# Output projection with five head pairs by seven products, small products in pieces of 32, and single-source mixer work on ScalarE

## The chip, the core and the metric

The kernel runs on one core of one Trainium2 chip. TensorE does the products, VectorE and ScalarE the elementwise work, GpSimd a few accumulating transfers, and SyncE's queue issues nearly all transfers. The metric is the device time of one execution in microseconds. Before the change the median of three runs is 973.27 us, from 970.83 to 974.09. A measurement of this kernel can tell a change of about 0.3%, some 2.9 us, from none.

## The reference

One decoder layer on 512 tokens of width 2048, behind 16 learned meta tokens; everything is float32:

```
x = rms_norm(input) ; p = x @ w_in                 # one projection, columns split among three mixers
A: gated DeltaNet, 6 heads x 128 (conv, SiLU, l2 norm, chunked delta rule)
B: GLA linear attention, 5 heads (dk 64, dv 128), key-dim gate, chunked
C: forgetting attention, 5 heads x 128, blocks of 128 queries
each head: o * silu(z)                             # A and B with a head norm first
y = concat(A 768, B 640, C 640) @ w_out + input    # one output projection, 2048 x 2048
out = rms_norm(y) without the meta tokens
```

The concatenated width is 16 heads of 128. The kernel counts it in eight **pairs** `kp` of two heads: pairs 0 to 2 are the DeltaNet heads, 3 and 4 the first four GLA heads, 5 is GLA head 4 with attention head 0, and 6 and 7 are the other four attention heads.

## The kernel before, in words

**Products.** Every large operand is split into a high and a low part (`wh`/`wl`, `oh`/`ol`, `sh`/`sl`): ScalarE copies the high part, VectorE subtracts it from the source to get the low one. A large product is then three matmuls (high by high, low by high, high by low), 128 rows by up to 512 columns. Products between small float32 tiles run without the split, and the trace has two matmuls for each of them.

**Order.** Every instruction is recorded at one line (L283, in `Weave.emit`) in an order that a planner at build time chooses. Each piece of work is a Python generator; what it yields, an operation or a list of operations, is emitted as a whole. The planner keeps a modelled clock for each engine, gives each generator a priority, and among those whose operands are modelled as ready takes the earliest. TensorE has two modes, full matmuls and small ones (fewer than 128 rows or 64 columns); the planner stays in the small mode for `LIGHT` us of modelled time and in the full one for at least `HEAVY`. `BACK` bounds how far the modelled transfer queue may run ahead of TensorE. On the chip every engine then executes its own list strictly in that order.

**Stages on TensorE.** The input projection's first columns (`pz`, `px`) run to about 540 us. From there to 823 us the three mixers are interleaved with the rest of the input projection (`pbfq`, `pbgz`, `pbfz`: 128x512 matmuls, the bulk that fills TensorE while a mixer's chains run on other engines) and with the first blocks of the output projection (`po`). The small products `pss` belong to GLA's decay levels: for each pair of heads, lists of 24 and three times 64 matmuls of 64x32 weights (`gla_levels`, L1388). In attention, `pfa`/`pfd` are scores, `fp` the probabilities, `pfw` their product with the values; the last of these waits for four small steps `mh` (ScalarE) and `ml` (VectorE).

**Output projection.** 512 tokens are four blocks of 128 (`tb`), 2048 columns four blocks of 512 (`cc`), summed in 16 accumulators `acc`. A block of one `cc` and one pair is 24 matmuls (`po`). For some pairs, the list `STK`, the 2x2 block product of two heads by two column blocks (or two token halves) is done by **seven products** instead of eight (`Seven`, L1701; `mm_seven`, L1829; Strassen's scheme): it needs sums of weight blocks, which transfers put together in DRAM (`osum`; GpSimd issues the accumulating ones, `out_sums`), and sums of head blocks (`os`, then `sh`/`sl`, in `seven_heads`). Each product ends with two additions into `acc` on VectorE (`seven_adds`). The order of the blocks is

```
PLAN = OUT + late[:1] + [SEV[0]] + late[1:2] + [SEV[1]] + late[2:] + [[Out(3, kp, True) for kp in [2] + LATE]]
```

`OUT` are eleven plain blocks of pairs 0 to 2, `SEV` the seven products for the two halves of the columns, `late` the plain blocks of pairs that are not in `STK`, and the last item (`mm_last`) does the remaining part of column block 3, token block by token block, on top of accumulators copied into `pz`.

**The end.** The output norm needs a whole row, so each token block needs all four columns: `square` (`sqf`, a square with a running sum on ScalarE) for each block, then `norm_out` (`frs`: a logarithm and an exponential of 128x1), then `scale_out` on ScalarE and VectorE, then the transfer to `out` on SyncE's queue. `weigh` multiplies an accumulator by the norm's weight ahead of that.

Of the kernel before, what the change touches and what calls it, by code (L numbers as in the profile page):

```python
# [8 lines left out]
F32 = mybir.dt.float32  # L9
# [4 lines left out]
AF = mybir.ActivationFunctionType  # L14
ALU = mybir.AluOpType
# [3 lines left out]
P = 128  # L19
D = 2048  # L20
KT = D // P
NM = 16
S = 512
T = NM + S
HT = T // 2
NB = S // P
EPS = 1e-6
H = 3
NN = NB * H
# [54 lines left out]
AP, KA, XP, GAP = -0.2, 2, 0.3, 0.1  # L84
BACK, BT = (3.0, 1.5), 100.0
LIGHT, SLACK, DMAL, STL = 2.0, 0.25, 1.1, 2.5
HEAVY, NEAR = 1.5, 0.05
KW = 2
NXP, SQP, NSL = -0.6, 0.0, 1.5
LP, LSL = 0.1, 1.0  # L90
WP, AOP, HDP = 1.0, -0.6, 0.0
EARLY_KP = ()
STK, KOS, OS0, OSN, OSP = (3, 4, 6, 7), 3, 1, 2, 0.1

# [266 lines left out]
def tile_hybrid_trunk(ctx, tc, xT, xtok, mtok, w_gate, w_first, w_in, w_out, consts, lmask, fin_w, out):  # L361
# [3 lines left out]
    V, A, G, PE, SP = (Engine(k, e) for k, e in zip("VAGPS", (nc.vector, nc.scalar, nc.gpsimd, nc.tensor, nc.sync)))  # L365
    pool = lambda n, es=ctx, **kw: es.enter_context(tc.tile_pool(name=n, bufs=1, reuse_waits="tile", **kw))
    VT = lambda out, in0, in1, op: V.scalar_tensor_tensor(out=out, in0=in0, scalar=1.0, in1=in1, op0=ALU.mult, op1=op)
# [3 lines left out]
    early, rows, mid, cps = ExitStack(), ExitStack(), ExitStack(), ExitStack()  # L371
# [163 lines left out]

    def silu_row(z, key, dst):
        if key[0] == "dz" or key in EARLY:
            yield A.activation(z, z, AF.Silu)
            yield SP.dma_start(out=dst, in_=z)
            return  # L540
        t = yield Get(row_s, f"st{key[0]}{key[1]}")
        yield V.tensor_scalar_max(t[:, :S], z, LOW)
        yield A.activation(t[:, :S], t[:, :S], AF.Exp, scale=-1.0)
        yield A.activation(t[:, :S], t[:, :S], AF.Ln, bias=1.0)
        yield A.activation(t[:, :S], t[:, :S], AF.Exp, scale=-1.0)
        yield VT(out=z, in0=z, in1=t[:, :S], op=ALU.mult)
        row_s.give(t)
        yield SP.dma_start(out=dst, in_=z)
# [174 lines left out]
    def token_rows(key, c, u):  # L723
# [30 lines left out]
        + [(("fk", h), ("fv", h)) for h in range(FOX_HEADS)]  # L754
    PAIRS = [p for c in zip(conv_pairs, other_pairs) for p in c]
    xpart = lambda k0, s: tuple((lambda j, t=t: t[k0 + j][:, s]) for t in (xh, xl))
    tpart = lambda d, s: tuple((lambda j, w=w: d[j // 2][w][:, j % 2, s]) for w in range(2))
# [80 lines left out]
    def store(p, n, u):  # L838
        yield VT(out=u, in0=u, in1=rstd, op=ALU.mult)
        key = p.keys[n]  # L840
        if key[0] in CONV:
            c = yield Get(row_s, f"cv{p.i}{n}")
            yield from conv(u, key, c, u)
            if key[0] != "dv":
                yield spilled(key, c)
            W.go(token_rows(key, c, u), -0.1, f"rows{key[0]}{key[1]}", 3.0)
        else:
            yield spilled(key, u)
            sp_of(key).set()
# [252 lines left out]
    def levels(g):  # L1102
# [6 lines left out]
        lh = [(slice(64 * q, 64 * q + 32), slice(64 * q + 32, 64 * q + 64)) for q in range(2)]  # L1109
        yield [PE.matmul(p3[lo_, n, :], an[hi_, n, lo_], uc[hi_, n, :], start=True, stop=True)  # L1110
               for n in range(NN) for lo_, hi_ in lh]
        m1 = yield Get(m_s, f"m1{g}", (P, NN, 32))
        for q in range(2):
# [3 lines left out]
        e_um[g].set()  # L1117
        yield [PE.matmul(p3[a, n, :], l[lo_, n, :], r[lo_, n, :], start=True, stop=True)
               for n in range(NN) for lo_, hi_ in lh for a, l, r in ((lo_, xc, m1), (hi_, m1, xc))]
        l1 = yield Get(m_s, f"l1{g}", (P, NN, 32))  # L1120
# [178 lines left out]
    SC = 1.0 / 16.0  # L1299
# [26 lines left out]
    def gla_load(p, ev):  # L1326
# [23 lines left out]
        for a in range(2):  # L1350
            yield V.tensor_scalar_add(u[:, a * HT : (a + 1) * HT], pg[a][:, :HT], bgk[:, p : p + 1])
            bank_s.give(pg[a])
# [12 lines left out]
    def gla_levels(p, group, sets, pair, at, a32, ev):  # L1365
# [8 lines left out]
        for s in group:  # L1374
# [12 lines left out]
            off += NB * n  # L1387
        yield mm  # L1388
        for s in group:
# [50 lines left out]
    def gla_pair(p, pair, sets, at):  # L1440
# [8 lines left out]
        d4 = dd[:, :S].rearrange("p (b t) -> p b t", b=NB)  # L1449
        yield VT(out=d4, in0=g4[:, :, P - 1 : P].to_broadcast([P, NB, P]), in1=g4, op=ALU.subtract)  # L1450
        yield A.activation(dd[:, :S], dd[:, :S], AF.Exp, scale=SC)
        yield VT(out=d4, in0=d4, in1=k4, op=ALU.mult)
# [168 lines left out]
    def fox_block(h, b, ld, phi, plo, mt, ev):  # L1621
# [24 lines left out]
        yield V.tensor_scalar_mul(m4[:, b, :NM], pr[:, :NM], sm[:, 0:1])  # L1646
        yield V.tensor_scalar_mul(pr[:, NM : m + P], pr[:, NM : m + P], sm[:, 0:1])
        yield [PE.transpose(pa[:, jb * P : (jb + 1) * P], pr[:, NM + jb * P : NM + (jb + 1) * P], ident)
# [167 lines left out]
    def seven_operands():  # L1816
        yield tuple(e_head[2 * kp] for kp in ST)
        for s in SEV:
            for n in ORDER:
                for kp in ST:  # L1820
                    src = yield s.src[kp, n]
                    hi = yield Get(d_s, f"wh{s.cp}{kp}{n}", (P, S), F32R)
                    lo = yield Get(d_s, f"wl{s.cp}{kp}{n}", (P, S), F32R)
                    yield A.copy(hi, src)
                    yield VT(out=lo, in0=src, in1=hi.bitcast(F32), op=ALU.subtract)
                    give(src, r_s, d_s)
                    s.op[n, kp].set((hi, lo))
# [271 lines left out]
```

## Time and profile before

| | before |
|---|---|
| median of the runs | 973.27 us (970.83 to 974.09, 3 runs) |
| profiled execution, its own time | 971.76 us |
| its span | 970.0 us, granted TensorE clock 0.995 |
| TensorE matmul busy | 947.7 us, 98% of the span |
| VectorE, ScalarE, GpSimd busy | 750.5, 569.6, 67.1 us |
| transfers | 167.18 MB, mean 172 GB/s |
| chain of work that ended last | TensorE 90%, VectorE 3%, ScalarE 3% |

The span is that of the instructions on the chip; 1.76 us of the run's time lie around it. Busy times come from one profiled execution. Idle time of an engine that nobody waits for costs nothing; where TensorE is idle, the row of waits says for whom.

### The profile page before, as it was taken

The page shows a single profiled execution, that of the slowest core. Times are in us where ns is not written, and L with a number is a line of the kernel's source. Part 1 is how long each engine was busy: PE and PEld are TensorE (multiplying, and loading weights), DVE is VectorE, ACT ScalarE, POOL GpSimd, SP SyncE. Part 2 cuts the span into 40 slices and gives each one's busy share as a digit, 9 for nine tenths or more (in the row PEclk, how much of TensorE's full clock was granted, in tenths as well). Part 3 has the DMA queues.
Part 4 walks back from the last instruction along what each step waited for, and adds up shares of the span by engine and source line. Part 5 has one row for each costly group of instructions (what it writes and reads, how often), then busy time and mean ns, then how long its engine had stood idle before and what let it go on. Part 6 is the DMA issues. An engine that isn't in the chain of part 4 may idle for free.

```text
span 970.0 us, 19077 instructions
## 1 busy us (share of the span) xinstructions
PE 947.7 (98%) x7283; PEld 844.5 (87%) x7283; DVE 750.5 (77%) x1337; ACT 569.6 (59%) x1205; POOL 67.1 (7%) x118
## 2 busy tenths in 40 slices
PE   9999999999999999999999999989989999999996
PEld 7888999999999999999987997778777787888885
DVE  7986887888888888798973666876866966888775
ACT  7865566667766576654424684637546565345445
POOL 0000101010100101110001111010010100000000
PEclk9999999999999999999999999999999999999999
DMA  9933648658784768692288335423233365474424
GB/s 344 372 113 132 164 136 226 191 150 228 193 228 117 220 154 253 171 229 83 89 290 292 97 88 182 141 85 137 99 100 135 107 207 182 154 261 153 151 67 173
DMA packets 92143, 167.18 MB, mean 172 GB/s; under 512 B 16253, under 2 KB 36477, under 8 KB 92052
## 3 DMA queue, kind: packets, MB, share of 16 engines
q1 hardware_dynamic: 87156, 157.31, 49.2%
q0 software_dynamic: 4608, 8.39, 6.5%
q8 instruction: 57, 0.93, 0.4%
q14 instruction: 34, 0.28, 0.1%
q10 hardware_dynamic: 288, 0.27, 0.1%
HBM read 142.33 MB, written 40.39 MB: 188 GB/s over the span
## 4 chain that ended last, share of the span: by engine, by line
PE 90%; DVE 3%; ACT 3%; issue 1%; DMA 1%; POOL 0%; SPq 0%; DVEq 0%; ACTq 0%; POOLq 0%
PE px L283 38%; PE po L283 9%; PE ps L283 8%; PE pz L283 5%; PE pbfq L283 5%; PE pbfz L283 5%; PE pbgz L283 4%; PE pbdz L283 2%; PE pbgq L283 2%; PE pg L283 1%; PE pss L283 1%; PE pfa L283 1%; PE pks L283 1%; PE pfw L283 1%; PE pgo L283 1%
## 5 line engine op out<-in xcount | busy, mean ns | idle before, releaser
L283 DVE SCALAR_TENSOR_TENSOR lp<-a,hp 128x1024 fp32r<-128x1024 f32 x90 | 110.7, 1231 | 36.9 <-ACT hp L283 36.1
L283 ACT CAST hp<-a 128x1024 fp32r<-128x1024 f32 x90 | 94.5, 1050 | 73.3 <-PE px L283 48.0
L283 PE MATMUL px<-xh,hp 128*128 128x264 f32 x432 | 123.7, 286 | 0.0
L283 PE MATMUL px<-xh,lp 128*128 128x264 f32 x432 | 122.7, 284 | 0.0
L283 PE MATMUL px<-xl,hp 128*128 128x264 f32 x432 | 122.7, 284 | 0.0
L283 PE MATMUL px<-tah,hp 128*128 128x264 f32 x288 | 83.8, 291 | 0.0
L283 PE MATMUL px<-tbh,hp 128*128 128x264 f32 x288 | 82.5, 287 | 0.0
L283 PE MATMUL px<-tbh,lp 128*128 128x264 f32 x288 | 82.3, 286 | 0.0
L283 PE MATMUL px<-tbl,hp 128*128 128x264 f32 x288 | 82.0, 285 | 0.0
L283 PE MATMUL px<-tah,lp 128*128 128x264 f32 x288 | 82.0, 285 | 0.0
L283 PE MATMUL px<-tal,hp 128*128 128x264 f32 x288 | 81.8, 284 | 0.0
L283 PEld LDWEIGHTS px<-xh,hp 128*128 128x128 f32 x432 | 81.4, 188 | 0.1
L283 PEld LDWEIGHTS px<-xh,lp 128*128 128x128 f32 x432 | 81.3, 188 | 0.0
L283 PEld LDWEIGHTS px<-xl,hp 128*128 128x128 f32 x432 | 81.2, 188 | 0.0
L283 PEld LDWEIGHTS px<-tbh,hp 128*128 128x128 f32 x288 | 54.3, 189 | 0.1
L283 PEld LDWEIGHTS px<-tah,hp 128*128 128x128 f32 x288 | 54.2, 188 | 0.1
L283 ACT CAST hp<-s 128x1024 fp32r<-128x1024 f32 x36 | 37.8, 1051 | 28.0 <-PE px L283 19.2
L283 PEld LDWEIGHTS px<-tal,hp 128*128 128x128 f32 x288 | 54.3, 188 | 0.0
L283 PEld LDWEIGHTS px<-tbl,hp 128*128 128x128 f32 x288 | 54.2, 188 | 0.0
L283 PEld LDWEIGHTS px<-tah,lp 128*128 128x128 f32 x288 | 54.2, 188 | 0.0
L283 PEld LDWEIGHTS px<-tbh,lp 128*128 128x128 f32 x288 | 54.2, 188 | 0.0
L283 DVE SCALAR_TENSOR_TENSOR lp<-s,hp 128x1024 fp32r<-128x1024 f32 x36 | 44.0, 1221 | 7.9 <-ACT hp L283 7.9
(406 smaller groups left out, 2642.2 us busy)
## 6 DMA issues: line engine op xcount, KB each, us to landing
a<-in_w_in SPq DMA_DIRECT2D x72, 512.0 KB, 5.7
osum<-in_w_out SPq DMA_DIRECT2D x32, 256.0 KB, 5.0
o<-in_w_out SPq DMA_DIRECT2D x16, 512.0 KB, 3.5
kd<-osum SPq DMA_DIRECT2D x25, 256.0 KB, 3.8
kd<-in_w_out SPq DMA_DIRECT2D x21, 256.0 KB, 4.2
rgz<-in_w_in SPq DMA_DIRECT2D x10, 512.0 KB
rfq<-in_w_in SPq DMA_DIRECT2D x10, 512.0 KB, 3.2
rfz<-in_w_in SPq DMA_DIRECT2D x10, 512.0 KB, 3.2
```

The source lines that it names most:

```text
L283: self.pin(op.call(*op.a, **op.kw))
```

## The change

Four things are edited, and the planner then makes a new order for the whole program.

1. `STK` takes pair 5 in: all five pairs of GLA and attention heads go by seven products. `LATE` becomes empty, so `PLAN` is `OUT`, `SEV[0]`, `SEV[1]`, and a last item of pair 2 alone. `osum` grows from 32 to 40 blocks; `OSN` goes from 2 to 1, so that the sums of consecutive pairs start one projection pair apart.
2. The lists of small products `pss` (64) and `pm` (48) are yielded in pieces of `CH = CD = 32`, `LIGHT` goes from 2.0 to 1.5 and the second value of `BACK` from 1.5 to 3.0.
3. Work with one tile as its source goes from VectorE to ScalarE: the bias of the GLA gate (`gu`), the decay of the keys (`gkd`, a subtraction and one exponential become a small copy and four exponentials with a bias), and the scaling of the attention probabilities (`fp`).
4. `EARLY_KP = (3, 4)` lets the splits and sums of pairs 3 and 4 start when GLA is done, in GLA's slots; `seven_operands` waits for `e_d` first, and for the heads of all pairs only ahead of the second product (`NOP = 1`).

`EXTRA` is empty and no pair of the list holds a `gz` or `fz` block, so the added branch in `store` and the argument `early` do nothing here.

```diff
-BACK, BT = (3.0, 1.5), 100.0
-LIGHT, SLACK, DMAL, STL = 2.0, 0.25, 1.1, 2.5
+BACK, BT = (3.0, 3.0), 100.0
+LIGHT, SLACK, DMAL, STL = 1.5, 0.25, 1.1, 2.5
...
+EXTRA = ()
+NOP, CH, CD = 1, 32, 32
 WP, AOP, HDP = 1.0, -0.6, 0.0
-EARLY_KP = ()
-STK, KOS, OS0, OSN, OSP = (3, 4, 6, 7), 3, 1, 2, 0.1
+EARLY_KP = (3, 4)
+STK, KOS, OS0, OSN, OSP = (3, 4, 5, 6, 7), 3, 1, 1, 0.1
...
-        yield [PE.matmul(p3[lo_, n, :], an[hi_, n, lo_], uc[hi_, n, :], start=True, stop=True)
-               for n in range(NN) for lo_, hi_ in lh]
+        mm = [PE.matmul(p3[lo_, n, :], an[hi_, n, lo_], uc[hi_, n, :], start=True, stop=True)
+              for n in range(NN) for lo_, hi_ in lh]
+        for i in range(0, len(mm), CD):
+            yield mm[i : i + CD]
...
-            yield V.tensor_scalar_add(u[:, a * HT : (a + 1) * HT], pg[a][:, :HT], bgk[:, p : p + 1])
+            yield A.activation(u[:, a * HT : (a + 1) * HT], pg[a][:, :HT], AF.Identity, bias=bgk[:, p : p + 1])
...
-        yield mm
+        for i in range(0, len(mm), CH):
+            yield mm[i : i + CH]
...
-        yield VT(out=d4, in0=g4[:, :, P - 1 : P].to_broadcast([P, NB, P]), in1=g4, op=ALU.subtract)
-        yield A.activation(dd[:, :S], dd[:, :S], AF.Exp, scale=SC)
+        gl = one((P, NB), f"ggl{p}")
+        yield A.activation(gl, g4[:, :, P - 1], AF.Copy, scale=SC)
+        for b in range(NB):
+            yield A.activation(d4[:, b], g4[:, b], AF.Exp, scale=-SC, bias=gl[:, b : b + 1])
...
-        yield V.tensor_scalar_mul(pr[:, NM : m + P], pr[:, NM : m + P], sm[:, 0:1])
+        yield A.activation(pr[:, NM : m + P], pr[:, NM : m + P], AF.Copy, scale=sm[:, 0:1])
...
-        yield tuple(e_head[2 * kp] for kp in ST)
+        yield e_d
         for s in SEV:
             for n in ORDER:
+                if n == ORDER[NOP]:
+                    yield tuple(e_head[2 * kp] for kp in ST)
                 for kp in ST:
```

TensorE has 5801 instructions in the program after it, 5819 before: 264 `po` matmuls instead of 336, 420 `ps` instead of 336, and 18 of 512 and 12 of 256 columns in the last item instead of 36 and 24. Three places of the order matter for what follows; `L283` and `L285` are the same recording line before and after.

TensorE, in the GLA levels of the first pair, where a list of `pss` ends (before) and where a piece ends (after); `pfa` are attention scores or transposes, `pbfz` the bulk. Before:

```order
L283 MATMUL pss_7521<-qx_6892,kx_6877 32x32
L283 MATMUL pss_7522<-qx_6892,kx_6877 32x32
L283 MATMUL pfa_7538<-fk_7012,fq_7014 128x144
L283 MATMUL pfa_7539<-fk_7012,fq_7014 128x272
L283 MATMUL pfa_7540<-fk_7012,fq_7014 128x400
L283 MATMUL pss_7630<-qx_6892,gkT_6917 32x32
L283 MATMUL pss_7631<-qx_6892,gkT_6917 32x32
```

After:

```order
L285 MATMUL pss_7576<-qx_6916,kx_6911 32x32
L285 MATMUL pss_7577<-qx_6916,kx_6911 32x32
L285 MATMUL pbfz_7551<-xh_204,hbfz_0_7373 128x512
L285 MATMUL pbfz_7551<-xl_205,hbfz_0_7373 128x512
L285 MATMUL pbfz_7551<-xh_204,lbfz_0_7374 128x512
L285 MATMUL pfa_7461<-ident,fp_7470 128x128 x2
L285 MATMUL pbfz_7551<-xh_255,hbfz_0_7373 128x512
L285 MATMUL pbfz_7551<-xl_256,hbfz_0_7373 128x512
L285 MATMUL pbfz_7551<-xh_255,lbfz_0_7374 128x512
L285 MATMUL pss_7576<-qx_6904,kx_6889 32x32
L285 MATMUL pss_7577<-qx_6904,kx_6889 32x32
```

Two lists of 64 stood three matmuls apart; now pieces of 32 stand apart by bulk, here by eight matmuls.

VectorE, between the last sums of head blocks (`sl`) and the low parts of the weights (`wl`) for the seven products; `acc<-acc,ps` adds a finished product, `acc<-acc,po` a finished block. Before:

```order
L283 SCALAR_TENSOR_TENSOR sl_9990<-os_9962,sh_9989 128x512
L283 SCALAR_TENSOR_TENSOR sl_9997<-os_9963,sh_9996 128x512
L283 SCALAR_TENSOR_TENSOR wl_10005<-kd_5908,wh_10004 128x512
L283 SCALAR_TENSOR_TENSOR wl_10010<-kd_5908,wh_10009 128x512
L283 TENSOR_TENSOR acc_9939<-acc_9939,po_9919 128x512
```

After:

```order
L285 SCALAR_TENSOR_TENSOR sl_10082<-os_10068,sh_10081 128x512
L285 SCALAR_TENSOR_TENSOR sl_10086<-os_10069,sh_10085 128x512
L285 TENSOR_TENSOR acc_9264<-acc_9264,ps_10009 128x512
L285 TENSOR_TENSOR acc_9268<-acc_9268,ps_10012 128x512
L285 SCALAR_TENSOR_TENSOR wl_10090<-kd_6140,wh_10089 128x512
```

The five low parts of the first product now stand far ahead (32 rows before the first of these), and the first low part of the second product stands behind the additions of the first product.

ScalarE, at the end; `pz` is the last item's PSUM, one tile for each token block, `frs` the norm. Before:

```order
L283 ACTIVATE sqf_10852,fss<-pz_10817 128x512
L283 ACTIVATE frs<-fss,frs 128x1
L283 ACTIVATE frs<-frs 128x1
L283 ACTIVATE acc_9338<-acc_9338,frs 128x512
L283 ACTIVATE acc_9798<-acc_9798,frs 128x512
L283 ACTIVATE sqf_10877,fss<-pz_10818 128x512
```

After:

```order
L285 ACTIVATE sqf_10902,fss<-pz_10881 128x512
L285 ACTIVATE sqf_10914,fss<-pz_10882 128x512
L285 ACTIVATE sqf_10925,fss<-pz_10883 128x512
L285 ACTIVATE sqf_10936,fss<-pz_10884 128x256
L285 ACTIVATE sqf_10946,fss<-pz_10885 128x256
L285 ACTIVATE frs<-fss,frs 128x1
L285 ACTIVATE frs<-frs 128x1
L285 ACTIVATE acc_9264<-acc_9264,frs 128x512
L285 ACTIVATE acc_9742<-acc_9742,frs 128x512
```

The norm of each token block followed its own square; now all five squares of the last item stand ahead of the first norm.

More of the change, by code (lines that the diff above doesn't have):

```diff
@@ L534, in tile_hybrid_trunk, with silu_row @@
     sp_of = lambda key: e_sp.setdefault(key, Ev())
-    def silu_row(z, key, dst):
-        if key[0] == "dz" or key in EARLY:
+    def silu_row(z, key, dst, early=False):
+        if early or key[0] == "dz" or key in EARLY:
             yield A.activation(z, z, AF.Silu)
@@ L755, in tile_hybrid_trunk @@
     PAIRS = [p for c in zip(conv_pairs, other_pairs) for p in c]
+    for i, p in EXTRA:
+        PAIRS.insert(i, p)
     xpart = lambda k0, s: tuple((lambda j, t=t: t[k0 + j][:, s]) for t in (xh, xl))
@@ L840, in store @@
         key = p.keys[n]
-        if key[0] in CONV:
+        if key[0] in ("gz", "fz"):
+            spill[key] = drp.tile([P, S], F32, name=f"sp{key[0]}{key[1]}")
+            yield from silu_row(u[:, NM:], key, spill[key], True)
+            sp_of(key).set()
+        elif key[0] in CONV:
             c = yield Get(row_s, f"cv{p.i}{n}")
@@ L1117, in levels @@
         e_um[g].set()
-        yield [PE.matmul(p3[a, n, :], l[lo_, n, :], r[lo_, n, :], start=True, stop=True)
-               for n in range(NN) for lo_, hi_ in lh for a, l, r in ((lo_, xc, m1), (hi_, m1, xc))]
+        mm = [PE.matmul(p3[a, n, :], l[lo_, n, :], r[lo_, n, :], start=True, stop=True)
+              for n in range(NN) for lo_, hi_ in lh for a, l, r in ((lo_, xc, m1), (hi_, m1, xc))]
+        for i in range(0, len(mm), CD):
+            yield mm[i : i + CD]
         l1 = yield Get(m_s, f"l1{g}", (P, NN, 32))
```

## The prediction

> **What bounds the kernel now.** I read the page's engine shares first, then TensorE's waits, then the chain that ended last.
>
> ```profile
> PE 947.7 (98%) x7283; PEld 844.5 (87%) x7283; DVE 750.5 (77%) x1337; ACT 569.6 (59%) x1205; POOL 67.1 (7%) x118
> ...
> q8 instruction: 57, 0.93, 0.4%
> ```
>
> TensorE is busy 98% of the span, so the time is the sum of its matmuls, the few stalls between them, and what follows its last one. The `q8` row is the queue that brings its instructions: 57 packets for 7283 matmuls and as many weight loads, 256 to a packet of 16 KB.
>
> ```profile
> PE pss L283 <- issue: 5.1, 3, 2.6
> PE pfw L283 <- DVE ml L283: 2.0, 3, 1.3
> PE pkd L283 <- DVE gst L283: 1.9, 2, 1.1
> ...
> PE pvf L283 <- DMA fv<-spfv: 0.7, 1, 0.7
> ...
> PE pvgv L283 <- DMA vgv<-spgv: 0.7, 1, 0.7
> PE pgo L283 <- ACT gon L283: 0.6, 1, 0.6
> ```
>
> These are TensorE's waits of 0.6 us and more that the edits touch. The largest is no wait for an engine: `issue` means that nothing the profile shows held the small products back. The timeline and a table of 5-us windows (engine columns, then granted clock, transfer share, GB/s) show it in place; the `q8` rows are those of the transfer view from 643.7 to 645 and from 718 to 719.5 us.
>
> ```profile
> 643.19 0.41 PE L283 MATMUL pss<-gqT,gkT 64*32 64x32 f32 x25
> 646.24 0.59 PE L283 MATMUL pss<-gqT,gkT 64*32 64x32 f32 x36 [2.64 <-issue]
> ...
> 720.73 0.43 PE L283 MATMUL pss<-gqT,gkT 64*32 64x32 f32 x34 [1.49 <-issue]
> ...
> 722.30 0.63 PE L283 MATMUL pbfz<-xh,hbfz 128*128 128x512 f32 x1
> 722.73 0.63 PE L283 MATMUL pbfz<-xl,hbfz 128*128 128x512 f32 x1
> ```
>
> ```profile
> 640.00:645.00 5.00, 3.56 (x209) 2.71 (x193) 2.61 (x14) 0.51 (x2) 0.27 (x1) 1.00 0.73 265
> 645.00:650.00 5.00, 3.76 (x44) 2.84 (x45) 2.64 (x14) 1.80 (x7) 0.85 (x3) 0.66 0.01 3
> 715.00:720.00 5.00, 4.24 (x111) 3.29 (x110) 2.57 (x8) 1.72 (x5) 0.00 (x0) 1.00 0.58 197
> 720.00:725.00 5.00, 4.27 (x45) 3.40 (x45) 1.82 (x6) 2.43 (x6) 0.00 (x0) 0.66 0.01 3
> ```
>
> ```profile
> q8 instruction: 1, 0.02, 4.4%
> ...
> q8 instruction: 1, 0.02, 3.9%
> ```
>
> TensorE stops in the middle of `pss` lists, and a packet of its instructions had come 1 to 2 us before each restart. A list of 64 is 128 matmuls in the trace and as many weight loads: exactly one packet, used up in little over 1 us, where the bulk takes a hundred times 0.232 us for the same number. So I read these stalls as TensorE running out of fetched instructions. Behind two of them the clock is granted at 0.66 over 5 us, and bulk matmuls start 0.43 us apart.
>
> ```profile
> 820.15 2.78 PE pfw L283 x14
> 822.93 38.98 PE po L283 x168
> 861.91 38.92 PE ps L283 x168
> ...
> 950.89 8.35 PE pz L283 x36
> ```
>
> In the chain, a 128x512 matmul takes 38.98 / 168 = 0.232 us, and after the last attention product 168 of them come ahead of the first of the seven products: 39 us of cover.
>
> **The products themselves.** 72 `po` fewer, 84 `ps` more, 18 fewer of 512 and 12 of 256 columns in the last item (half of 0.232 each): 12 matmuls of 0.232 us fewer, **-2.8 us**, all on the path. The eight more plain loads and eight more accumulating transfers of `osum` run under the input projection, at a mean of 172 GB/s; I cost them at nothing. If a load came late it would hold a product back by a transfer, which none of the waits above shows.
>
> **The pieces.** The two orders show six more groups of `pss`, so twelve more edges between small and full matmuls.
>
> ```profile
> 814.28 0.48 PE L283 MATMUL po<-ho,oh 128*128 128x512 f32 x1
> 814.60 0.40 PE L283 MATMUL po<-lo,oh 128*128 128x512 f32 x1
> ```
>
> Behind a small one the next full matmul starts 0.32 us later instead of 0.23: 0.09 an edge, **+1.0**. The stalls should mostly go, since counted over the new order (0.232 us for a full matmul, 0.009 for a small one in a burst) 256 instructions take at least 3.8 us; but the first two pieces of the first pair are still only three `pfa` apart, and the window from 715 to 720 us shows that 221 instructions in 5 us are enough for a stall, not only the 402 from 640 to 645. I take **-5.0** of 5.1 and the 0.6 that row of waits misses (bounds -5.7 and 0). Half clock goes with its stalls: each window is 3.4 us at half speed, by the clock 0.66 over 5 us (5 x 0.34 x 2 = 3.4), so it costs 1.7; two cost 3.4, **-3.3** (bounds -3.3 and 0).
>
> [...]
>
> **ScalarE instead of VectorE.** VectorE (77%) and ScalarE (59%) are both off the path but inside the mixers' chains. For `gkd` a 512-wide subtraction of about 0.68 us and one exponential become a small copy and four exponentials of 128 columns.
>
> ```profile
> L283 ACT ACTIVATE gon<-pgo x20: 258/282/318, 654.3 to 788.2; 128x128 f32<-128x128 f32 x20
> L283 ACT CAST mh<-pfw x20: 237/256/260, 622.4 to 819.5; 32x128 fp32r<-32x128 f32 x20
> L283 DVE TENSOR_TENSOR ml<-pfw,mh x20: 272/286/298, 623.7 to 819.8; 32x128 fp32r<-32x128 f32 x20
> ```
>
> By the `gon` row the four cost 1.1 us, as much as what they replace: nothing on a chain. What changes the waits is the new order, since bulk is spread differently. `pfw` waits for four rounds of `mh` and `ml`, 4 x 0.54 = 2.2 us and handovers. In the new order 18, 12, 24 and 20 bulk matmuls (2.8 us or more) stand there for four heads, but behind the last head nine as before: of the 2.0 us the 1.3 stay, -0.7. `pvf` and `pvgv` get their loads earlier, past a load that waited for VectorE, and more bulk ahead: -1.2 of 1.4 and of a third small wait. `pkd` -0.6, `pgo` of the first pair, with twelve bulk matmuls of cover instead of some 22, +0.5; small ones -0.3. Together **-2.3** (bounds -4 and +2, the latter if one chain, which the order does not time, comes 2 us late).
>
> **The start of the seven products.** Only 72 `po` are left as cover, 16.7 us.
>
> ```profile
> L283 DVE SCALAR_TENSOR_TENSOR sl<-os,sh x8: 681/686/694, 826.9 to 854.2; 128x512 fp32r<-128x512 f32 x8
> L283 DVE SCALAR_TENSOR_TENSOR wl<-kd,wh x46: 681/691/695, 854.8 to 935.5; 128x512 fp32r<-128x512 f32 x46
> L283 DVE TENSOR_TENSOR acc<-acc,po x28: 676/679/689, 806.3 to 950.9; 128x512 f32<-128x512 f32 x28
> ```
>
> VectorE has, behind the last `pfw`, five `wl`, six `ol`, eight additions, twelve halves of `os` at 0.42 and six `sl`, about 24.5 us with what it waits for; then the two additions of the first product, and only then the second product's first `wl`. TensorE needs that after 72 `po` and 30 `ps`, 102 x 0.232 = 23.7 us; it comes at 24.5 + 1.3 + 0.7 = 26.5. **+2.6**. The floor is the second addition alone, which cannot start before the first product's end: 0.6 + 0.7, so +1.2; +4 if the queue is 1.4 us later than I counted. A stall of this size can bring half clock, as those of 2.64 and 1.49 did and another of 0.98 did not: half of 1.7, **+0.8**. Queued behind this `wl` are the other four of the product, each 0.69 us for six matmuls of 1.4 us: TensorE does not stall twice.
>
> [...]
>
> **The end.** The last item is halved, and its squares all stand ahead of the first norm on ScalarE.
>
> ```profile
> L283 PE MATMUL pz<-ho,ol x20: 278/391/397, 951.2 to 961.8; 128*128 128x512 f32 x12, 128*128 128x256 f32 x8
> L283 SPq DMA_DIRECT2D out<-acc x16: 332/396/487, 955.6 to 965.4; - x16
> 962.41 0.20 ACT L283 ACTIVATION_READ_ACCUMULATOR sqf<-pz 128x1 f32 x1
> 963.05 0.29 ACT L283 ACTIVATE frs<-fss,frs 128x1 f32<-128x1 f32 x1 [0.44 <-DVE frs L283]
> 963.61 0.72 ACT L283 ACTIVATE acc<-acc,frs 128x512 f32<-128x512 f32 x1
> 955.00:960.00 5.00, 5.00 (x28) 4.21 (x26) 3.33 (x9) 4.58 (x12) 0.00 (x0) 1.00 0.76 255
> 960.00:965.00 5.00, 2.06 (x18) 1.85 (x16) 3.51 (x10) 3.76 (x11) 0.00 (x0) 1.00 1.02 360
> 965.00:970.00 5.00, 0.00 (x0) 0.00 (x0) 0.02 (x1) 0.00 (x0) 0.00 (x0) 0.73 0.62 224
> ```
>
> TensorE ends at 961.8 + 0.28 = 962.1, 7.9 us before the span's end. The first transfer out was issued 6.5 us before that, at 955.6, and 4.2 MB (5 us at 255, 360 and 224 GB/s) left by 970.0: 14.4 us, with the transfer share at 1.02 in the middle, so the stream was the bound. Now the first norm starts when the last square is read, 0.5 us after TensorE's end; norm and first scaling take 1.3 us. First issue 1.8 us after TensorE's end, end of the stream 14.4 later: 16.2 instead of 7.9, **+8.3** (bounds +7 and +9.5: VectorE's twelve operations left then take some 8.5 us, less than the stream).
>
> **Sum.** -2.8 + 1.0 - 5.0 - 3.3 - 2.3 + 2.6 + 0.8 + 8.3 = -0.7 us against a span of 970.0: 969.3. The profiled execution took 971.76, 1.76 more than its span, and lies 1.5 under the median: 972.5 on the median's scale. By the 0.3%, "no change" is from 970.35 to 976.2.
>
> **Rivals.**
>
> *The losses are smaller than counted (faster).* The five early `wl` let VectorE reach the second product in time but for the floor, no half clock follows, every mixer wait shrinks to its bound, and the stream at the end starts at +7: -1.4 - 0.8 - 1.7 - 1.3 = -5.2, **967.3**. For it: 98% busy, and VectorE has 20 instructions fewer. Against: the end's order is in the program, not in a count of mine. Chance 0.37.
>
> *The stalls stay (slower).* The packet is used up too fast even in pieces, at the two pieces that stand three `pfa` apart and where four or six matmuls part two others: 5.0 + 3.3 on top, **980.8**. From 3.7 us of these 8.3 on, the kernel is slower. For it: the stall behind a window with only 221 instructions in 5 us. Against: of the eight lists of 24 and 64 only three stalled, so most bursts are covered by what was fetched ahead. Chance 0.22, with a late seven products at +4 and half clock as the smaller part.
>
> *The pieces do nothing at all.* A list whose pieces are taken one after the other is the list before; the order shows this for `pm` (48 in a row), not for `pss`. Then the stalls stay as well: in the 0.22.
>
> The forecast, no change, has 0.41. The range takes in the faster rival's 967.3 with a bound more, 966, and two thirds of the way to the slower one's 980.8, 978.5; the forecast's own range is 970.35 to 976.2.
>
> **What would show it.** Right: no `issue` row over 1 us in TensorE's waits and no 5-us window under 0.9 of clock between 600 and 760 us; a wait of `ps` for `wl` of 1 to 4 us at the second product; the first `out` issue 1.5 to 2.2 us after TensorE's last matmul, and 16 us from there to the end. Wrong: an `out` issue before TensorE's end, since then 8.3 us of loss are not there, or `pss` rows with `issue` of 2 us, since then the gain is not.

## The result

The change made the kernel slower by 0.7%: 980.7 us, the median of 20 runs (977.06 to 985.22), against 973.79 us (20 runs). The ratio is 1.0071, with a 95% interval from 1.0054 to 1.0088. The forecast was 972.5, no change, and the range ended at 978.5. The profiled execution of the changed kernel took 981.58 us, with a span of 979.8.

The page's engine shares and TensorE's waits after the change:

```profile
PE 949.6 (97%) x7265; PEld 842.9 (86%) x7265; DVE 740.4 (76%) x1311; ACT 580.2 (59%) x1250; POOL 71.8 (7%) x126
```

```profile
PE pg L285 <- DMA an<-spdk: 3.1, 3, 1.9
PE pfw L285 <- DVE ml L285: 2.4, 3, 1.8
PE pm L285 <- DVE uc L285: 1.7, 1, 1.7
PE ps L285 <- DVE wl L285: 1.5, 1, 1.5
PE pgo L285 <- ACT gon L285: 1.2, 2, 0.6
PE warm L285 <- POOL ones L285: 1.1, 1, 1.1
PE pkd L285 <- DVE gst L285: 1.0, 2, 0.8
PE ps L285 <- ACT wh L285: 0.5, 1, 0.5
```

No `issue` row is left: the stalls inside `pss`, 5.1 us in the row before, are gone. At the top stands a row that was not there: `pg`, products of DeltaNet's keys, waits for loads of a spilled tensor (`an<-spdk`). The first and last starts of TensorE's tiles show where the 9.8 us of span arose:

| start of, us | before | after | difference grows by |
|---|---|---|---|
| first `px` | 93.3 | 94.2 | +0.9 |
| first `pm` | 518.7 | 525.3 | +5.7 |
| first `pbfz` | 584.4 | 590.4 | -0.6 |
| first `ps` (with 5.6 us of `po` fewer ahead of it) | 861.7 | 856.5 | -11.2 |
| last item (8.4 us of `ps` and `po` more ahead of it) | 950.7 | 957.9 | +12.4 |
| end of TensorE (last item halved) | 962.1 | 963.7 | -5.6 |
| end of the span | 970.0 | 979.8 | +8.2 |

From the first `pbfz` to the last item the kernel gained 1.6 us net of the matmuls moved (-11.2 + 5.6 + 12.4 - 8.4), where the terms of the prediction for these stages add up to -6.2. The end costs 8.2, as predicted. The largest part that no term has is lost before the first `pm`, in the input projection: 6.6 us. Of these the 0.9 ahead of the first `px` is scatter: e2 and e6 below have the same order on TensorE and in SyncE's queue up to the first `pm`, and their first `px` starts at 93.5 and 94.5 us. The rows below are the loads, the landing times of the transfers on `an` from 180 to 400 us, and the windows (engine columns, granted clock, transfer share, GB/s) of that first part, before:

```profile
L283 SPq DMA_DIRECT2D an<-spdk x30: 415/432/1806, 210.5 to 384.4; - x30
...
DMA to landing us min/median/max: 2.6/3.7/5.3
...
200.00:250.00 50.00, 50.00 (x417) 49.79 (x416) 43.65 (x56) 36.77 (x81) 4.31 (x6) 1.00 0.68 178
```

After:

```profile
L285 SPq DMA_DIRECT2D an<-spdk x30: 320/433/1346, 192.3 to 342.6; - x30
...
DMA to landing us min/median/max: 2.4/5.4/8.6
...
200.00:250.00 50.00, 48.07 (x395) 47.31 (x395) 39.36 (x52) 35.17 (x78) 6.97 (x9) 1.00 0.81 215
300.00:350.00 50.00, 48.77 (x401) 48.33 (x400) 43.30 (x53) 33.24 (x53) 6.83 (x9) 1.00 0.84 230
```

The new order puts these products and the loads they need earlier, the loads by 11 to 42 us, into a stretch with more transfers (a share of 0.81 instead of 0.68 from 200 to 250 us), where they take longer to land: 5.4 us in the median instead of 3.7, and up to 8.6 instead of 5.3. The end, after the change:

```profile
L285 SPq DMA_DIRECT2D out<-acc x16: 332/422/1147, 965.5 to 976.0; - x16
...
964.08 0.19 ACT L285 ACTIVATION_READ_ACCUMULATOR sqf<-pz 128x1 f32 x1
964.17 0.28 ACT L285 ACTIVATE frs<-fss,frs 128x1 f32<-128x1 f32 x1
...
965.00:970.00 5.00, 0.00 (x0) 0.00 (x0) 5.00 (x10) 4.35 (x10) 0.00 (x0) 0.56 0.72 251
970.00:975.00 5.00, 0.00 (x0) 0.00 (x0) 2.22 (x6) 1.37 (x4) 0.00 (x0) 0.50 1.06 367
```

TensorE ends at 963.7, the last square is read at 964.3, the first transfer out is issued at 965.5, and the stream takes 14.3 us from there.

### The profile page after: what moved, and what is told of

It reads as the page before. It is cut to its first block, busy times and chain, and to the rows that moved or that the text cites. A ratio compares the mean times of both kernels' runs of the same rounds, so it can differ in the third digit from the quotient of the medians.

```text
span 979.8 us, 19114 instructions
## 1 busy us (share of the span) xinstructions
PE 949.6 (97%) x7265; PEld 842.9 (86%) x7265; DVE 740.4 (76%) x1311; ACT 580.2 (59%) x1250; POOL 71.8 (7%) x126
## 5 line engine op out<-in xcount | busy, mean ns | idle before, releaser
L285 DVE SCALAR_TENSOR_TENSOR lp<-a,hp 128x1024 fp32r<-128x1024 f32 x90 | 110.1, 1224 | 36.9 <-ACT hp L285 36.5
L285 ACT CAST hp<-a 128x1024 fp32r<-128x1024 f32 x90 | 94.4, 1049 | 62.0 <-PE px L285 42.0
L285 PE MATMUL px<-xh,hp 128*128 128x264 f32 x432 | 124.5, 288 | 0.0
L285 PE MATMUL px<-xl,hp 128*128 128x264 f32 x432 | 122.8, 284 | 0.0
L285 PE MATMUL px<-xh,lp 128*128 128x264 f32 x432 | 122.8, 284 | 0.0
L285 PE MATMUL px<-tah,hp 128*128 128x264 f32 x288 | 83.0, 288 | 0.0
L285 PE MATMUL px<-tbh,hp 128*128 128x264 f32 x288 | 82.5, 286 | 0.0
L285 PE MATMUL px<-tbh,lp 128*128 128x264 f32 x288 | 82.0, 285 | 0.0
L285 PE MATMUL px<-tbl,hp 128*128 128x264 f32 x288 | 81.9, 284 | 0.0
L285 PE MATMUL px<-tah,lp 128*128 128x264 f32 x288 | 81.9, 284 | 0.0
L285 PE MATMUL px<-tal,hp 128*128 128x264 f32 x288 | 81.8, 284 | 0.0
L285 PEld LDWEIGHTS px<-xh,hp 128*128 128x128 f32 x432 | 81.4, 188 | 0.1
L285 PEld LDWEIGHTS px<-xl,hp 128*128 128x128 f32 x432 | 81.3, 188 | 0.0
L285 PEld LDWEIGHTS px<-xh,lp 128*128 128x128 f32 x432 | 81.2, 188 | 0.0
L285 DVE SCALAR_TENSOR_TENSOR wl<-kd,wh 128x512 fp32r<-128x512 f32 x65 | 43.9, 690 | 25.2 <-PE ps L285 20.9
L285 ACT CAST wh<-kd 128x512 fp32r<-128x512 f32 x65 | 39.7, 618 | 36.3 <-PE ps L285 30.9
L285 DVE SCALAR_TENSOR_TENSOR lp<-s,hp 128x1024 fp32r<-128x1024 f32 x36 | 44.0, 1223 | 17.8 <-ACT hp L285 17.7
L285 PEld LDWEIGHTS px<-tbh,hp 128*128 128x128 f32 x288 | 54.3, 188 | 0.1
L285 PEld LDWEIGHTS px<-tah,hp 128*128 128x128 f32 x288 | 54.3, 188 | 0.0
L285 PEld LDWEIGHTS px<-tbl,hp 128*128 128x128 f32 x288 | 54.3, 188 | 0.0
L285 PEld LDWEIGHTS px<-tal,hp 128*128 128x128 f32 x288 | 54.2, 188 | 0.0
L285 PEld LDWEIGHTS px<-tbh,lp 128*128 128x128 f32 x288 | 54.2, 188 | 0.0
```

The costliest lines, as they stand in the source:

```text
L285: self.pin(op.call(*op.a, **op.kw))
```

## The experiments

All ratios are to the kernel before on the same chip, with a 95% interval.

### The end

e1: the priority of `weigh`, one number.

```diff
-WP, AOP, HDP = 1.0, -0.6, 0.0
+WP, AOP, HDP = 0.0, -0.6, 0.0
```

> The change with one number altered: the priority of the norm's weights (weigh) from 1.0 to 0.0. TensorE's and SyncE's orders stay the same; on ScalarE each token block's norm follows its own square again, and VectorE's multiplications by the weights move ahead. Theory (the end costs 8.2 us because no norm can start before TensorE's end): the first transfer out is issued some 5 us before TensorE's end, the rest behind TensorE's last matmul falls from 16.1 to 9 to 11 us, and the time falls by 5 to 7 us, to 974 to 976. Rival (the stream out is slow by itself, or VectorE's twelve operations are what is late): less than 2 us.

977.75 us, 1.0060 (1.0033 to 1.0087): 3 us less than the change in microseconds, but the two were measured apart, and against the kernel before the change has 1.0071, so that the time alone shows no gain clear of the noise. The profile does. TensorE's last matmul and the transfers out:

```profile
L285 PE MATMUL pz<-ho,ol x10: 281/392/393, 959.1 to 964.2; 128*128 128x512 f32 x6, 128*128 128x256 f32 x4
L285 SPq DMA_DIRECT2D out<-acc x16: 332/404/870, 962.4 to 971.5; - x16
...
PE pg L285 <- DMA an<-spdk: 5.6, 2, 3.4
```

The first transfer leaves 2 us ahead of TensorE's end, not 5, and 11.9 us remain behind it instead of 16.1. So the order of squares and norms is 4.2 us of the 8.2; it came from `weigh` standing too late in VectorE's queue. The other 4.0 are the halved last item itself: the stream needs 14 us from the first norm on, the first norm needs one token block of the item, 1.4 us instead of 2.8, and the rest of the item lies under the stream either way. The theory was right in kind and too large: the first issue came 2 us and not 5 ahead of TensorE's end, and 11.9 us stayed where 9 to 11 were expected. The last row is scatter: with the orders of TensorE and of SyncE's queue unchanged up to the first `pm`, the waits for `spdk` were 5.6 us in this execution, with a half-clock window behind them, and 3.1 in that of the change.

### The loss before the first `pm`

e2 sets the second value of BACK back to 1.5; e3 takes pair 5 out of the seven products again; e10 does both.

```diff
-BACK, BT = (3.0, 3.0), 100.0                                    # e2, e10
+BACK, BT = (3.0, 1.5), 100.0
-STK, KOS, OS0, OSN, OSP = (3, 4, 5, 6, 7), 3, 1, 1, 0.1         # e3, e10
+STK, KOS, OS0, OSN, OSP = (3, 4, 6, 7), 3, 1, 2, 0.1
```

> The change with the second value of BACK at 1.5 again, so that the modelled transfer queue runs ahead of TensorE no further than in the kernel before; osum's transfers as in the change. First theory (osum's sixteen more transfers in a denser order delay the loads of DeltaNet's operands): TensorE still waits 2 to 4 us for an<-spdk, and the first pm starts at 524 to 526 us. Second theory (BACK lets the planner put loads behind a longer queue and TensorE's use of them too close): these waits are under 0.6 us and the first pm starts at 519.5 to 522 us.

> The change without its first part: pairs 3, 4, 6 and 7 go by seven products, the sums two pairs apart as before; pieces, ScalarE's work, BACK and LIGHT as in the change. First theory (osum's transfers delay the loads): no wait for an<-spdk over 0.6 us, first pm at 519.5 to 522 us. Second theory (BACK does): waits of 2 to 4 us stay and the first pm is at 524 us or later. Later stages: 2.8 us more matmuls; with plain products of pair 5 between, the seven products start without a wait.

> The kernel without pair 5 (e3) with the second value of BACK at 1.5: the fourth corner of the square of BACK and pair 5 (the change, e2 and e3 are the others). Theory (BACK costs only where osum's transfers are dense): no wait of pg for spdk, first pm within 1.5 us of e3's 521.3, time within 2 us of 964.5. Rival (3.0 for BACK is worth something by itself without pair 5): 2 us or more slower than e3, or as much faster where it costs.

e2: 975.31 us, 1.0024 (0.9997 to 1.0051). e3: **964.50 us, 0.9910 (0.9881 to 0.9939)**, the fastest kernel of the study. e10: 969.72, 0.9970 (0.9925 to 1.0015). The first `pm` and the loads, of e2, and the first `pm` of e3:

```profile
519.01 0.95 PE L285 MATMUL pm<-uc,an 32*32 32x32 f32 x48 [0.53 <-DVE uc L285]
...
L285 SPq DMA_DIRECT2D an<-spdk x30: 320/432/1540, 210.5 to 357.9; - x30
```

```profile
521.29 0.95 PE L285 MATMUL pm<-uc,an 32*32 32x32 f32 x48 [1.28 <-DVE uc L285]
```

Neither theory of e2 and e3 is right alone: each single undoing takes the waits for `spdk` away. Two settings together make the planner ask for the loads at 192 us: `BACK` at 3.0, which lets it run transfers further ahead, and the sums that came with pair 5. Not all of e2's gain stays: from the first `pm` to the first `pbfz` e2 takes 73.6 us and e6, with the same order, 69.2, against 65.1 in the change. Each has a stall on `issue` in a list of `pm` there, of 1.6 and 1.3 us, and e2 two half-clock intervals behind it.

In e10 the rival held: without pair 5 the kernel is 5 us slower with `BACK` at 1.5 than at 3.0 (four runs, on another chip than e3). It loses them late. From the first `pbfz` to the first `ps` it takes 267.6 us against 265.6 in e3, and from there to the last item 93.3 against 91.0, with 2.4 us of waits at the start of the seven products (1.5 of them in e3 too) and a half-clock window. So `BACK` at 3.0 costs only together with the sums, and without them it helps; why the later order is better is not shown.

e9 keeps e3's 32 blocks of sums and puts them one projection pair apart; e13 keeps the change's 40 and puts them 1.6 apart.

```diff
-STK, KOS, OS0, OSN, OSP = (3, 4, 6, 7), 3, 1, 2, 0.1            # e9, against e3
+STK, KOS, OS0, OSN, OSP = (3, 4, 6, 7), 3, 1, 1, 0.1
-STK, KOS, OS0, OSN, OSP = (3, 4, 5, 6, 7), 3, 1, 1, 0.1         # e13, against the change
+STK, KOS, OS0, OSN, OSP = (3, 4, 5, 6, 7), 3, 1, 1.6, 0.1
-            p, q = pairs[OS0 + OSN * i : OS0 + OSN * i + 2]
+            p, q = pairs[int(OS0 + OSN * i) : int(OS0 + OSN * i) + 2]
```

> The kernel without pair 5 (e3), but with OSN = 1: the same 32 blocks of osum, their sums one projection pair apart as in the change, so that as many transfers a microsecond run as there until the 32 are done. Theory A (the density of the sums, with BACK at 3.0, is what makes the loads of DeltaNet's operands late): waits of pg for an<-spdk of 2 us or more together, first pm 2 to 4 us later than in e3, time 966 to 969. Theory B (it is the number of transfers, eight plain and eight accumulating more): no such wait over 0.6 us, time within 1.5 us of e3's 964.5.

> The change with the sums of its ten blocks spread: 1.6 projection pairs apart instead of 1 (BACK 3.0, five pairs, all else as in the change), so that they end about where they end in the kernel before. Theory (the density of the sums, as e9 showed for 32 blocks, is what makes the change's loads late too): waits of pg for spdk under 0.8 us together instead of 3.1, first pm at 520 to 522.5 us instead of 525.3, time 976 to 978. Rival (forty blocks are too many at any spacing): first pm at 524 us or later, time 979 to 982.

e9: 976.46 us, 1.0044 (0.9996 to 1.0092), 12 us behind e3. e13: 978.22, 1.0028 (0.9988 to 1.0069). Waits and loads of e9, then waits and first `pm` of e13:

```profile
PE pg L285 <- DMA an<-spdk: 6.8, 4, 2.7
...
L285 SPq DMA_DIRECT2D an<-spdk x30: 319/444/1881, 192.4 to 344.3; - x30
```

```profile
PE px L285 <- DVE u L285: 1.6, 2, 1.4
...
523.33 1.19 PE L285 MATMUL pm<-uc,an 32*32 32x32 f32 x48 [1.62 <-DVE uc L285]
```

With `BACK` at 3.0 density is enough: with no block more, `OSN` at 1 brings the early loads (192.4) and the waits back, and more of them than in the change. The first `pm` of e9 starts at 532.3 us, 11.0 later than in e3, so nearly all its loss lies there. Both theories had the time more than 7 us too low; three intervals of half clock behind the waits, 10.2 us in all and so some 5 us of loss, came on top. Its profiled execution is also the slowest of its four. Spread out, forty blocks no longer make TensorE wait for `spdk`, but 1.6 us for VectorE's `u` come in and the first `pm` stands 2.0 us earlier than in the change, between the two theories.

Several kernels have the same order, on TensorE and in SyncE's queue, up to the first `pm`, so that their profiles show how much this stage scatters:

| same order up to the first `pm` | first `px` to first `pm`, us |
|---|---|
| before, e7, e10, e12 | 425.4, 426.4, 426.4, 426.7 |
| the change, e1, e4 | 431.1, 434.6, 433.1 |
| e2, e6 (`BACK` at 1.5) | 425.5, 424.9 |
| e3, e5, e8, e11 (no pair 5) | 427.6, 426.8, 426.8, 425.6 |
| e13, e14 (sums spread) | 429.6, 429.8 |
| e9 (no pair 5, sums dense) | 438.7 |

In e2 and e6 three bulk matmuls (0.7 us) fewer stand ahead of the first `pm`, and in e3, e5, e8 and e11 three more. The change's three executions lie above all others but e9. On average they lose 6.7 us here against the first row, and the density of the sums is about 3 of them; what of the rest is the number of transfers and what the new order is not told apart.

### The pieces

e4 is the change with lists of 64 (`CH, CD = 64, 64`); e7 the kernel before with pieces alone.

```diff
+CH = 32                                                          # e7, against the kernel before
-LIGHT, SLACK, DMAL, STL = 2.0, 0.25, 1.1, 2.5
+LIGHT, SLACK, DMAL, STL = 1.5, 0.25, 1.1, 2.5
-        yield mm
+        for i in range(0, len(mm), CH):
+            yield mm[i : i + CH]
```

> The change with lists of 64 instead of pieces of 32 (CH = CD = 64); the order is the same up to the first decay lists at about 620 us. Theory (a list of 64 uses up a packet of 256 instructions faster than the next one comes): waits of pss with no releaser return, 3 to 6 us in two or three places, with one or two windows of half clock at 1.7 us each; time 4 to 8 us longer than the change. Rival (the stalls went with something else of the change, LIGHT or ScalarE's work): no such wait over 0.5 us, time within 2 us of the change.

> The kernel before with only the pieces: pss in lists of 32 and LIGHT 1.5, which lets the planner put bulk between them (with LIGHT at 2.0 it takes them one after the other). Everything up to about 520 us is as before. Theory (the stalls and the clock behind them are lists of one whole packet): no issue wait of pss over 0.5 us, no half clock between 600 and 760 us, time 5 to 9 us under before, 964 to 968. Rival (pieces alone only move the loss into edges and other waits): less than 3 us.

e4: 986.23 us, 1.0125 (1.0082 to 1.0169). e7: 967.64, 0.9956 (0.9939 to 0.9974). The wait rows, first e4's, then e7's:

```profile
PE pss L285 <- issue: 3.7, 2, 2.5
```

```profile
PE pss L284 <- issue: 1.7, 2, 1.4
```

Pieces alone bring the kernel before 4.6 us, and its stage from the first `pbfz` to the first `ps` is 5.5 us shorter (271.8 instead of 277.3). That lists of 64 stall TensorE more than pieces of 32 holds both ways: the `pss` row of `issue` is 5.1 us before and 1.7 in e7, 3.7 in e4 and none in the change. What they cost the change is less clear: by the medians e4 is 5.5 us slower, with four runs of which one took 999.88, but in the profiles the same stage takes 266.8 us against 266.1, and 1.9 of the 2.7 us of longer span arose ahead of it, where the two have the same order. In e7 one stall of 1.4 us stayed, with no half clock, where the theory had none over 0.5; with the stalls in e2's and e6's `pm` (1.6 and 1.3 us), which is in pieces too, pieces had fewer stalls here, not none.

### The work on ScalarE

e8 is e3 with the three moves of part 3 undone; e11 is e3 with only the probabilities on ScalarE; e12 is e7 with all three (the lines are those of the change's diff).

> The kernel without pair 5 (e3) and with the gate's bias, the keys' decay and the scaling of the probabilities on VectorE as before; pieces, BACK and LIGHT as in e3. Theory (neither engine is on the path there and the chains are as long): within 2 us of e3's 964.5. Rival (VectorE's queue was what held kst, ml and the operands back): 3 to 6 us slower than e3, with waits of pkd, pfw and pss for VectorE.

> The kernel without pair 5 (e3) and with only the scaling of the attention probabilities on ScalarE; the gate's bias and the keys' decay on VectorE again. e8 with all three on VectorE took 970.2 and waited 3.2 us for fp from VectorE. Theory (the scaling is what TensorE's transposes wait for): most of the 5.7 us between e8 and e3 is back, 964.5 to 966.5, and no wait of pfa for fp over 0.6 us. Rival (the keys' decay or the bias holds the rest, or the new order as a whole does): 967.5 to 970.

> The kernel before with the pieces (LIGHT 1.5) and the work on ScalarE, and nothing else of the change: no pair 5, BACK, EARLY_KP and seven_operands as before. e7 (pieces alone) took 967.6, and ScalarE's work is worth 5.7 us by e3 and e8. Theory (the two add up, and early operands bring nothing): 962 to 964, the fastest. Rival (the early operands are part of e3's gain): 965 to 968.

e8: 970.21 us, 0.9984 (0.9972 to 0.9996). e11: 966.83, 0.9938 (0.9894 to 0.9982). e12: 970.80, 0.9987 (0.9939 to 1.0034). Rows of TensorE's waits of e8, of e11, and of e12:

```profile
PE pfa L285 <- DVE fp L285: 3.2, 3, 1.3
PE pkd L285 <- DVE gst L285: 1.4, 2, 1.0
...
PE pkd L285 <- DVE gkd L285: 1.0, 1, 1.0
```

```profile
PE pfa L285 <- ACT fp L285: 0.7, 1, 0.7
```

```profile
PE ps L284 <- ACT wh L284: 2.2, 1, 2.2
PE ps L284 <- DVE wl L284: 1.3, 1, 1.3
```

On e3 the moves are worth 5.7 us, where I had said nothing: with the pieces' order, TensorE waited 3.2 us for VectorE's scaling of the probabilities and 2.4 for the keys' decay and states (0.9 in e3). Of the 5.7, the probabilities' scaling alone has 3.4, a little less than its theory had. e12 should have been the fastest and was slower than both its theory and its rival: the same three moves, on e7, cost 3.2 us (0.9956 to 0.9987). So what they are worth depends on the order around them, and 5.7 is no property of the moves. At the seven products e12 has 3.5 us of waits and half clock, which the early operands (part 4) might have saved. But e10, which differs from e12 by part 4 and the pieces of `pm`, has 2.4 us of waits and half clock there too and is only 1.1 us faster on the same chip, four runs each: a share of part 4 in e3's gain is not shown.

### The start of the seven products, and five pairs mended

e5 is e3, and e6 and e14 are the change, with the weights' splits ahead of the additions; e6 has e2's and e1's numbers besides, e14 e13's and e1's.

```diff
-        W.go(seven_operands(), -0.45, "sops")
+        W.go(seven_operands(), -0.65, "sops")
```

> The kernel without pair 5 in the seven products (e3) with one number altered: the weights' splits (seven_operands) at priority -0.65 instead of -0.45, ahead of the additions (-0.6). TensorE's order is the same to the last row; on VectorE the second product's first low part now stands ahead of the first product's additions. Theory (the wait of 1.5 us at the second product is the additions in front of wl): no wait of ps for wl over 0.4 us, time 1.5 to 2 us under e3's 964.5, 962.5 to 963. Rival (VectorE is late by its whole queue, so that the order of these few rows decides nothing): the wait stays over 1 us, or the same time comes back as another wait of ps.

> The change with its five pairs and the three settings mended that cost it time: the second value of BACK at 1.5, weigh at 0.0, seven_operands at -0.65. From e2's 975.3: 4.1 us for the end as in e1, nothing at the seven products, where e2 had no wait. Theory (the half of the last item that was saved lay under the stream out, so five pairs bring at most the 2.8 us fewer matmuls less some 4 us at the end): 970 to 972.5, still behind e3's 964.5. Rival (with its orders mended the fifth pair is worth its 2.8 us): 962 to 965.

> As e13, and weigh at 0.0 (as in e1) and seven_operands at -0.65 (as in e5, e6). Theory (five pairs with all their side costs mended still lose at the end what they save, since half of the last item lay under the stream out): 968 to 972, behind e3's 964.5. Rival (mended, five pairs are worth their 2.8 us): 961 to 965, the fastest.

e5: 965.88 us, 0.9941 (0.9918 to 0.9964). e6: 971.54, 0.9990 (0.9969 to 1.0010). e14: 971.98, 0.9972 (0.9946 to 0.9999). Waits of e5, then TensorE's last matmul and the transfers out of e14:

```profile
PE ps L285 <- DVE acc L285: 1.4, 1, 1.4
...
PE ps L285 <- DVE wl L285: 0.5, 2, 0.3
```

```profile
L285 PE MATMUL pz<-ho,ol x10: 277/392/397, 952.8 to 957.8; 128*128 128x512 f32 x6, 128*128 128x256 f32 x4
L285 SPq DMA_DIRECT2D out<-acc x16: 333/410/725, 956.1 to 965.7; - x16
```

In e5 the wait for `wl` shrank to 0.5 us and one for the additions, which now stand behind, came: VectorE is late by its queue there, not by the order of two rows, and nothing was gained. With everything mended in two different ways, five pairs come to 971.5 and 972.0, 7 us behind four pairs. Between e13 and e14, on one chip, the order at the end and the splits are worth 6.2 us, and what stands behind TensorE's end falls from 16.2 to 11.9. e14's profile has 11.9 us behind TensorE's end, 4.1 more than e3's 7.7, so what the last item gave up stays lost, and behind the last attention head nine `po` stand ahead of `pfw` where e3's order has fifteen, so that 1.8 us of its wait stay, as in the change.

## Why the prediction was wrong

**What bounds the kernel** held: 97% busy after, and the larger differences could be found as waits of TensorE, as half clock or at the end.

**The products themselves**: -2.8, and the count of matmuls held. But the sentence that costed the transfers of `osum` at nothing, under a mean of 172 GB/s, is the step that failed. It asked whether sixteen more transfers fit under the mean rate, not what the denser sums and `BACK` do to the order of the loads around them. Shown: 6.6 us lost before the first `pm`, all but 0.9 of them behind the first `px`, where loads that land later than before make TensorE wait; e2 and e3 take most of it away, e9 brings it back by `OSN` alone. `BACK` had no price in the prediction at all, although the diff has it, and its 3.0 is the other half of this loss.

**The pieces**: the stalls went, -5.7 for my -5.0. The edges were probably undersized: when the `po` that moved, the stalls, one half-clock window fewer and the listed waits are taken from the -11.2 of the stage from the first `pbfz` to the first `ps`, +3.2 us are left, not 1.0. I put them down to small gaps between unlike matmuls, an estimate that no run separates. The half clock was as large an error: -3.3 and +0.8 in my sum. Two windows were there again, behind the wait for `ml` and behind the one at the seven products:

```profile
832.48:835.89 3.41, 1.64 (x7) 1.05 (x6) 1.44 (x5) 1.86 (x6) 0.00 (x0) 1.00 0.92 297
835.89:839.30 3.41, 3.41 (x13) 3.08 (x12) 1.22 (x1) 3.41 (x8) 0.00 (x0) 0.50 0.55 186
863.20:866.61 3.41, 1.36 (x5) 0.59 (x4) 3.41 (x6) 1.94 (x4) 0.00 (x0) 1.00 0.81 231
866.61:870.02 3.41, 3.41 (x10) 2.63 (x9) 1.39 (x3) 0.62 (x1) 0.00 (x0) 0.50 0.93 336
```

The windows moved from the stalls that were mended to waits that had been or had become as long, -0.2 instead of -2.5.

**ScalarE instead of VectorE**: I said nothing on a chain and -2.3 for the waits by the new order. Apart from the stalls, the rows of waits in that stage went from 6.5 to 5.1 us, -1.4; `pfw` rose to 2.4 instead of falling to 1.3. The reason was wrong: e8 shows that without the moves the kernel of four pairs takes 5.7 us longer. I had compared chains instruction by instruction and not the queue on VectorE that they leave.

**The start of the seven products**: +2.6 predicted; the waits rows have 1.5 and 0.5, and 2.5 us are lost from start to start. Right in size, though e5 shows that the additions ahead of `wl` are not what decides.

**The end**: +8.3 predicted, +8.2 measured, and the first issue 1.8 us after TensorE's end as said. What I did not see is that half of it comes from the smaller last item: the -2.8 and the +8.3 belong together, and on four pairs neither is there.

**The rivals.** The slower one was to come from stalls that stay; slower it was, by another way, and that its 980.8 stands next to the measured 980.7 is chance. Lists of 64 stalled in the kernel before and in e4, 5.1 and 3.7 us on `issue`, and pieces with bulk between them did not stall in the change. That the stalls are the fetch is read from when the packets came, one between 643.7 and 645 us and one between 718 and 719.5, ahead of the restarts at 646.24 and 720.73; no run shows it by itself. In sum the prediction lacks 10.5 us: 6.6 before the first `pm`, 2.3 for the clock, 2.2 for the edges, 0.9 for the mixers' waits, less 0.7 for the stalls, 0.6 between `pm` and `pbfz`, and 0.1 each at the seven products and the end.

## What to carry to other kernels

When a change adds transfers that nobody waits for, look up in the order which loads move because of them, and which engine waits for those; the mean rate, 172 GB/s before and 177 after, said nothing on that here. Work saved in the last stage, under a stream of results that is the bound there, was not saved here: the stream took 14.4 us before and 14.3 after, and the halved item lost 4.0 us at the end. So save it elsewhere or make the stream start earlier. When a bundle of edits comes out slower, take it apart: here three parts together are worth some 8 us, and the fourth, which has the bundle's only saved matmuls, costs 16. The parts do not add up one by one: the same three moves gained 5.7 us in one order and cost 3.2 in another.

## What the hardware showed that I had not expected

The half clock fell in intervals of 3.413 us on a grid that was fixed within an execution: in the change the two begin at 835.89 and 866.61, nine intervals apart, in the kernel before at 646.46 and 721.56, 22 apart. In these profiles half clock followed more often the less TensorE had streamed in one interval of the grid. In the change, 1.36 and 1.64 us of matmul busy out of 3.41, which leave 2.1 and 1.8 us without a matmul, were followed by it. In e1 the first of the same waits left 1.65 us and was not; the second fell across the border of two intervals, with 2.81 and 1.96 busy, and was not either:

```profile
836.28:839.69 3.41, 1.65 (x8) 1.05 (x7) 1.44 (x5) 1.85 (x7) 0.00 (x0) 1.00 0.89 268
839.69:843.10 3.41, 3.41 (x19) 2.97 (x19) 2.10 (x3) 3.41 (x7) 0.00 (x0) 1.00 0.61 207
863.58:866.99 3.41, 2.81 (x12) 1.74 (x10) 3.31 (x8) 2.36 (x5) 0.00 (x0) 1.00 0.31 99
866.99:870.41 3.42, 1.96 (x8) 1.61 (x9) 2.68 (x6) 1.06 (x2) 0.00 (x0) 1.00 0.91 290
```

The grid of e1 is taken from its own half-clock window, 351.58 to 354.99 us. In all sixteen profiles, from 60 to 955 us, the nine intervals with at most 1.54 us busy (0.77 in the kernel before, 0.92 in e4) were all followed by half clock; of those with 1.64 to 2.15 some were (1.92 in the kernel before, 2.14 in e3) and some were not (1.65 and 1.96 in e1, 1.77 in the change). So a wait of 1.5 to 2 us was near the edge here, and whether it cost 1.7 us more, half of 3.413, depended also on where it fell in the grid, which differs from run to run.

Half clock lasted in e3's profiled execution: a wait of 1.3 us ahead of `pm` was followed by three half intervals in a row, and `pm`, with the bulk between its lists, took 18.3 us from first to last start instead of 11.3 in the change, though TensorE counts as busy all along:

```profile
519.91:523.33 3.42, 2.14 (x54) 1.83 (x54) 1.86 (x3) 1.19 (x3) 0.00 (x0) 1.00 0.99 245
523.33:526.74 3.41, 3.41 (x12) 1.87 (x11) 0.58 (x1) 0.47 (x1) 0.00 (x0) 0.50 0.62 173
526.74:530.15 3.41, 3.41 (x101) 2.50 (x101) 0.00 (x0) 0.27 (x1) 0.00 (x0) 0.50 0.99 389
```

That execution took 969.67 us, 5.2 above the median of its kernel. In e13 a wait of 1.6 us ahead of `pm` was followed by one half interval only. In e3 the first half interval holds 1.4 us of products of 16 rows (`pym`), in e13 it holds the rest of a `pm` list and bulk; why half clock lasted in the one and not in the other is not shown.
